# A two-layer hybrid decoder trunk: order of evacuations, last x sums and value transposes around a gated recurrence, and the place of one convolved tile

## The chip, the cores and the metric

The kernel runs on 1 core of one Trainium2 chip, as one launch. The time is device microseconds of that core; lower is better. The engines are TensorE (PE, with its weight loads PEld), VectorE (DVE), ScalarE (ACT), GpSimd (POOL) and SyncE (SP, which issues most DMAs). Each works through its own instructions in order; semaphores make one wait for another. Matmuls write to PSUM banks of 128x512 float32; DVE or ACT must empty a bank before it is used again.

## The reference

Input x is 1024 tokens by 1024 features, float32. Layer 0 mixes tokens with a gated linear recurrence (HGRN2, 8 heads of 128); layer 1 with sliding-window attention. Each layer then has a gated FFN (2816 wide) with a causal depthwise convolution of width 3, and layer norms after each part.

```python
q, f, i, g = split(h @ w_in, 4)
fg = lb + (1 - lb) * sigmoid(f)                 # forget gate; k = 1 - fg, v = i
o  = hgrn2_chunkwise(silu(q), 1 - fg, i, log(fg))   # S_t = diag(f_t) S_{t-1} + k_t v_t^T ; o_t = S_t^T q_t
o  = rmsnorm(o) * g_norm_w * silu(g)
h  = layer_norm(ALPHA * h + o @ w_out)
u  = causal_conv3(h @ ffn_w_in) + conv_b        # per channel
a, b = split(u, 2)
h  = layer_norm(ALPHA * h + (silu(a) * b) @ ffn_w_out)
```

## The kernel before

**Precision and products.** Every large matmul works on float32 split in two parts, hi (an ACT cast, L249, L874, L1298) and lo (a DVE subtraction, `low_part`, L197): hi x hi, hi x lo, lo x hi, the three matmuls of `mm3` (L222 to L224). Large products are cut by Strassen's scheme with seven products and sums of blocks of the weights and of x. A product here is 12 matmuls of 128x512 (four k blocks times three).

**The order.** PE's order, and in the recurrence that of ACT, DVE and SP too, is the order in which the program issues. `Order` (called `od`) keeps a model clock `od.t`, which each matmul advances, and a model of DVE's backlog, `od.v`. Side work is written as generators: `od.spawn(task, delay)` sets one up, `od.tick()` after each k block runs those whose time has come, `yield t` pauses one, `od.behind(us, least)` is the pause until DVE's backlog is done, and `od.finish` runs tasks to their end at once. A tick also calls a hook that issues weight casts on ACT (`cast_next`), and a filler that issues low parts on DVE (`job_next`).

**The recurrence.** Head 0's q, f, i and g are projected first; `ig_block` computes values and gates of row blocks tb = 4 to 7 (`tp` 2 and 3). Then `line` lists 98 products (m, p): pair m = 0 to 13 stands for head h = 1 to 7 and g = 0 (its q and f) or g = 1 (its gates and values), p is the Strassen product. A block of the line reads (m,1), (m-1,3), (m-1,4), (m,6), (m,5), (m,2), (m,7). The line starts with (0,1), (0,2), (0,6), (0,5), (0,7) and ends with (13,7), (13,3), (13,4). `product(n)` makes weights ahead, issues the 12 matmuls with a tick behind each of the four k blocks, and then spawns and steps `evacuate`, which empties the bank: p = 1, 6, 5 and 4 by an ACT copy (L1380, L1382, L1384, L1386), p = 2, 7 and 3 by a DVE add (L1392) and then an activation. Four banks serve the line: 1 for p = 2, 2 for p = 5 and 3, and 0 or 3 (by m's parity) for the others, so (13,4) uses the bank of (13,7).

**x sums.** The right operands of some products are sums of x's blocks. Those of product p = 5 are written by `last_sums(0)` over T's first four k blocks, columns 512 and up, which `ig_block` reads; its four row blocks each take an ACT cast (L874) and a DVE low part (L197). It is spawned after the last i/g block and finished before product (0,5). `opened` says how far along the line weights may be cast.

**The chain.** `all_heads` runs `recur(h)` for head after head: seven doubling levels (`update`, L1116 and L1118) with bursts of small matmuls into `psax` tiles (two of them, two banks each), `put`s that copy the scores to A; then k is transposed to kd (ACT copy L1187), and, for h > 0, the head's values, which the line leaves transposed, are turned by eight transposes and an ACT copy (L1196); then the state updates KV = kd, V (into psax), the states St on DVE, and the outputs. The chain waits until `values_in[0]` has reached h, which `evacuate` sets with (m,4) of g = 1. `norm` follows per head (L1235, L1239, L1248).

**The FFN.** `Up.run` goes over 22 columns fc of the up-projection, each with seven products. `collect` adds them up in Y, and for p = 4 and p = 3 runs the convolution of the a and b half: ACT writes the scaled u into a tile c (L526), DVE adds two shifted terms (L528, twice), and then c of the a half goes through SiLU (L531) and the b half is multiplied in (L533; on POOL for fc < 2, on DVE after) and stored to `gd`. The tile of the a half is row 4 or 5 of Y, that of the b half row 6 (Y6). `weight_load` (L471) brings a column's raw weights as two tiles r1 and r2 from a ring; for fc = 3 the second, r2, is row 7 of Y (Y7), as for each second column from then on. `weight_sums` makes sums of them (L480 to L483) and splits them (L249, L197). In the FFN only PE's order is the program's; the others are placed by the framework's scheduler, which keeps all dependences in program order: a load into a tile waits for earlier users of that tile.

## Time and profile before

| | us |
|---|---|
| median of 3 runs | 2119.31 |
| lowest, highest | 2119.15, 2119.46 |
| the profiled execution | 2119.05 |
| its span, first to last instruction | 2117.3 |
| PE busy in it | 2087.5 |
| DVE, ACT, POOL busy | 1777.7, 972.3, 189.0 |
| mean granted TensorE clock | 0.996 |

The recurrence's line of products runs from 63.1 to 435.9 us of the span, the first columns of layer 0's FFN from 554.6, those of layer 1's from 1490.9.

How to read the rows: a timeline row is start, duration, engine, line of the program, operation, tiles written<-read, shape, count, and in brackets the engine's idle time before it and what ended it. A row of waits is the engine with the waiting tile and line, what it waited for, the total, the number and the longest. A window's row is its bounds and length, busy time and count of PE, PEld, DVE, ACT, POOL, then the clock granted to TensorE (1.00 is full), the share of the DMA engines that was busy, and GB/s. PE's matmuls overlap, so their rows last longer than their distance.

### The profile page before, as it was taken

The numbers are of one execution on the slowest core, as the hardware profiler recorded it, in microseconds if no ns is written. First come the engines' busy times: TensorE is split into PE (matmuls) and PEld (weight loads), VectorE is DVE, ScalarE is ACT, GpSimd is POOL, SyncE is SP. The second block draws the span as 40 slices with busy tenths as digits, with TensorE's granted clock in tenths as the row PEclk, the third lists the DMA queues.
The fourth block names the chain that finished last, engine by engine and source line by source line (L and its number), as shares of the span: only waits on it lengthen the run. The fifth ranks groups of instructions, "written<-read, shape, count | busy, mean of one in ns | idle before, by whom it ended". The sixth has DMA issues, their size and how long they took to land. (4 is left out here: it accounts for less than half of the span.)

```text
span 2117.3 us, 31595 instructions
## 1 busy us (share of the span) xinstructions
PE 2087.5 (99%) x12303; PEld 1737.2 (82%) x12303; DVE 1777.7 (84%) x2420; ACT 972.3 (46%) x1586; POOL 189.0 (9%) x214
## 2 busy tenths in 40 slices
PE   9899999999999999999999999999999999999998
PEld 8688888877878888888888888888888888888886
DVE  6777777759989989887988668979999999978986
ACT  6555655543444444443533366743544444444430
POOL 1000000001010000000001122311010000000002
PEclk9999999999999999999999999999999999999999
DMA  4021111333247765628754511052266776449662
GB/s 153 21 70 51 51 51 51 100 135 109 90 124 183 185 163 149 160 93 297 261 189 159 159 35 37 24 159 91 88 169 165 176 178 160 120 154 325 224 207 100
DMA packets 239823, 286.82 MB, mean 135 GB/s; under 512 B 30216, under 2 KB 160440, under 8 KB 239416
## 3 DMA queue, kind: packets, MB, share of 16 engines
q1 hardware_dynamic: 223360, 238.26, 34.8%
q0 software_dynamic: 15456, 46.16, 11.0%
q8 instruction: 97, 1.59, 0.3%
q14 instruction: 54, 0.44, 0.1%
q10 hardware_dynamic: 856, 0.37, 0.1%
HBM read 241.72 MB, written 89.15 MB: 156 GB/s over the span
## 5 line engine op out<-in xcount | busy, mean ns | idle before, releaser
L222 PE MATMUL psmm<-T,HL 128*128 128x512 f32 x816 | 323.4, 396 | 7.9 <-ACT T L874 4.8
L223 PE MATMUL psmm<-T,HL 128*128 128x512 f32 x816 | 319.4, 391 | 1.2 <-DVE T L197 1.2
L224 PE MATMUL psmm<-T,HL 128*128 128x512 f32 x816 | 319.3, 391 | 0.2 <-DVE HL L197 0.2
L528 DVE SCALAR_TENSOR_TENSOR Y<-Y,cwt,Y 128x1023 f32<-128x1023 f32 (+1 forms) x176 | 225.2, 1281 | 50.8 <-ACT Y L526 49.4
L249 ACT CAST HL<-rx 128x1024 fp32r<-128x1024 f32 (+1 forms) x151 | 151.3, 1007 | 164.1 <-PE psmm L223 29.0
L197 DVE TENSOR_TENSOR HL<-rx,HL 128x1024 fp32r<-128x1024 f32 (+1 forms) x151 | 176.4, 1175 | 16.5 <-ACT HL L249 16.3
L222 PEld LDWEIGHTS psmm<-T,HL 128*128 128x128 f32 x816 | 153.9, 189 | 40.3 <-ACT T L874 5.2
L224 PEld LDWEIGHTS psmm<-T,HL 128*128 128x128 f32 x816 | 153.9, 189 | 33.0 <-DVE HL L197 0.6
L223 PEld LDWEIGHTS psmm<-T,HL 128*128 128x128 f32 x816 | 154.1, 189 | 32.8 <-DVE T L197 2.2
L222 PE MATMUL psax<-T,HL 128*128 128x512 f32 x392 | 152.9, 390 | 0.0
L223 PE MATMUL psax<-T,HL 128*128 128x512 f32 x392 | 152.6, 389 | 0.0
L224 PE MATMUL psax<-T,HL 128*128 128x512 f32 x392 | 152.5, 389 | 0.0
L526 ACT ACTIVATE Y<-Y,cwt 128x1024 f32<-128x1024 f32 x88 | 108.8, 1237 | 93.5 <-DVE Y L515 83.5
L197 DVE TENSOR_TENSOR HL<-raw,HL 128x512 fp32r<-128x512 f32 (+1 forms) x121 | 92.3, 789 | 45.7 <-ACT HL L1298 35.6
L271 POOL TENSOR_TENSOR rs<-rs,nhalf 128x1 f32<-128x1 f32 x32 | 45.0, 1406 | 735.7 <-DVE rs L270 735.7
L249 ACT CAST HT<-rx 128x1024 fp32r<-128x1024 f32 (+1 forms) x37 | 35.5, 960 | 135.0 <-DVE rx L482 67.4
L222 PE MATMUL psmm<-HL 128*128 128x512 f32 x220 | 86.6, 394 | 0.0
L222 PEld LDWEIGHTS psax<-T,HL 128*128 128x128 f32 x392 | 73.7, 188 | 15.3 <-DVE Y L509 0.2
L224 PEld LDWEIGHTS psax<-T,HL 128*128 128x128 f32 x392 | 73.6, 188 | 15.4
L223 PEld LDWEIGHTS psax<-T,HL 128*128 128x128 f32 x392 | 73.5, 188 | 15.1
L224 PE MATMUL psmm<-HL 128*128 128x512 f32 x220 | 85.7, 390 | 0.0
L223 PE MATMUL psmm<-HL 128*128 128x512 f32 x220 | 85.7, 390 | 0.0
(404 smaller groups left out, 5194.7 us busy)
## 6 DMA issues: line engine op xcount, KB each, us to landing
rx<-in_ffn_w_in_dram SPq DMA_DIRECT2D x136, 256.0 KB
rx<-gd SPq DMA_DIRECT2D x118, 256.0 KB
bsd<-in_ffn_w_out_dram POOLq DMA_DIRECT2D x36, 768.0 KB, 8.6
gd<-Y SPq DMA_DIRECT2D x44, 512.0 KB
raw<-in_hgrn_w_in_dram SPq DMA_DIRECT2D x30, 512.0 KB
rx<-in_ffn_w_out_dram SPq DMA_DIRECT2D x54, 256.0 KB
R<-bsd SPq DMA_DIRECT2D x44, 256.0 KB
Y<-in_ffn_w_in_dram SPq DMA_DIRECT2D x40, 256.0 KB
```

The lines of the kernel that those rows point to most:

```text
L197: make = lambda e: e.tensor_tensor(lo, src, hi.bitcast(F32), op=ALU.subtract)
L222: nc.tensor.matmul(ps, st(0), mv(0), start=start, stop=False, skip_group_check=onto)
L223: nc.tensor.matmul(ps, st(0), mv(1), start=False, stop=False, skip_group_check=onto)
L224: nc.tensor.matmul(ps, st(1), mv(0), start=False, stop=stop, skip_group_check=onto)
L249: nc.scalar.copy(hi, src)
L271: nc.gpsimd.tensor_tensor(rs, rs, nhalf, op=ALU.pow)
L526: nc.scalar.activation(c, u, AF.Identity, bias=cwt[:, l, 3, ci:ci + 1], scale=cwt[:, l, 2, ci:ci + 1])
L528: nc.vector.scalar_tensor_tensor(c[:, sh:], u[:, :S - sh], cwt[:, l, 2 - sh, ci:ci + 1], c[:, sh:], op0=ALU.mult, op1=ALU.add)
```

## The change

- `collect`: for fc = 1 the convolved tile of the b half is Y7; for all others it stays Y6.
- `ig_block` takes a callback, and the last x sums are spawned row block by row block, each behind the i/g block that last reads its part of T. `opened` is set to the whole line after the first product.
- `product`: the tick behind a product's last k block comes after the first step of that product's evacuation. For pair 0 the activation behind a DVE add pauses 5.0 at least, where it paused 0.8.
- `recur`: the values are no longer turned in the chain; the pause behind kd is 2.6 (2.0 for the last two heads), where it was 2.8. `turn_values(h)` does it as a task of its own, 3.0 behind the evacuation of the values' last part, and sets `values_in`.

```diff
--- before.py
+++ after.py
@@ -522,7 +522,7 @@
                 part = 0 if p == 4 else 1
                 ci = fc + part * NF
                 u, ca = C[:, part, :], Y[:, 4 + fc % 2, :]
-                c = Y[:, 6, :] if part else ca
+                c = Y[:, 7 if fc == 1 else 6, :] if part else ca
                 nc.scalar.activation(c, u, AF.Identity, bias=cwt[:, l, 3, ci:ci + 1], scale=cwt[:, l, 2, ci:ci + 1])
                 for sh in (1, 2):
                     nc.vector.scalar_tensor_tensor(c[:, sh:], u[:, :S - sh], cwt[:, l, 2 - sh, ci:ci + 1],
@@ -772,7 +772,7 @@
             nc.scalar.copy(vg[:, 0], pv[:, :, 0, :])
             yield 0.0
 
-        def ig_block(h, us, tp, ahead=None):
+        def ig_block(h, us, tp, ahead=None, behind=None):
             if ahead:
                 ps = psmm()
                 first_rows(us, ps, ahead)
@@ -788,6 +788,8 @@
                     od.tick()
                 soon.append(od.spawn(values(tb, ps)))
                 gated.setdefault(h, []).append(soon[-1])
+                if behind:
+                    behind(tb)
                 od.tick()
 
         def soon_all(left=0):
@@ -864,9 +866,9 @@
                 low_part(t[:, 1], src, t[:, 0], None)
                 od.vec(0.7)
 
-        def last_sums(part):
-
-            for i in range(4):
+        def last_sums(part, blocks=range(4)):
+
+            for i in blocks:
                 ts = slice(i * P, (i + 1) * P)
                 t, src = (TXs[1][:, :, :, ts], xf[i][:, 512:]) if part else (
                     T[:, :, :4, 512 + i * P:512 + (i + 1) * P], s1[:, i])
@@ -1185,16 +1187,10 @@
             put()
             kd = hp.tile([P, S], F32, name="kd")
             nc.scalar.copy(kd, ps)
-            yield 2.8
+            yield 2.6 if h < NH - 2 else 2.0
             while values_in[0] < h:
                 yield 0.2
             V = VG[h][:, 0, :].rearrange("p (c d) -> p c d", c=NB)
-            if h:
-                ps = psax()
-                for c in range(NB):
-                    tr(ps[:, c * P:(c + 1) * P], V[:, c, :])
-                nc.scalar.copy(VG[h][:, 0, :], ps)
-                yield 2.2 if h < NH - 2 else 1.3
             ps = psax()
             for c in range(NB - 1):
                 cs = slice(c * P, (c + 1) * P)
@@ -1218,6 +1214,15 @@
                     mm32(ps[:, cs], qp[:, cs], St[:, c, :], start=False)
             values_done[0] = h
             normed.append(od.spawn(norm(h, ps.rearrange("p (c t) -> p c t", c=NB))))
+
+        def turn_values(h):
+
+            ps = psax()
+            for c in range(NB):
+                tr(ps[:, c * P:(c + 1) * P], VG[h][:, 0, c * P:(c + 1) * P])
+            nc.scalar.copy(VG[h][:, 0, :], ps)
+            values_in[0] = h
+            yield 0.0
 
         def norm(h, pv):
 
@@ -1384,7 +1389,7 @@
                 nc.scalar.copy(second[:, late], ps)
             elif p == 4 and g:
                 nc.scalar.copy(first[:, late], ps)
-                values_in[0] = h
+                od.spawn(turn_values(h), 3.0)
             elif p == 4:
                 forget(h, first, kp, late, ps)
             else:
@@ -1392,7 +1397,7 @@
                 tt(to[:, half], to[:, half], ps, op=add)
                 od.vec(0.7)
                 taken.append(1)
-                yield od.behind(0.1, 0.8)
+                yield od.behind(0.1, 0.8 if m else 5.0)
                 if p != 2:
                     nc.scalar.activation(to[:, half], to[:, half], AF.Silu)
                 elif g == 0:
@@ -1414,12 +1419,14 @@
             for k in range(4):
                 od.t += 0.031
                 mm3(ps, lambda j: w[:, j, k * P:(k + 1) * P], lambda j: moving[p](j, k), k == 0 and p in (1, 2, 5), k == 3, onto=p in (6, 7, 3, 4))
-                od.tick()
+                if k < 3:
+                    od.tick()
             done[0] = n + 1
             taken = []
             readers[b] = od.spawn(evacuate(m, p, ps, taken)), taken
             evacs.setdefault(m, []).append(readers[b][0])
             od.step(readers[b][0])
+            od.tick()
 
         values_done, normed = [-1], []
         wo = a["hgrn_w_out"][0]
@@ -1486,17 +1493,17 @@
                     yield from recur(h, *args)
 
             task = od.spawn(all_heads(), 0.5)
+            firsts = []
             for tp in range(2, 4):
-                ig_block(0, us, tp)
-            opened[0] = len(line)
-            firsts = od.spawn(last_sums(0), 0.2)
+                ig_block(0, us, tp, behind=lambda tb: firsts.append(od.spawn(last_sums(0, [tb - 4]), 0.1)))
             soon_all()
             banks = [psmm() for _ in range(4)]
             lead, moved = 1, []
             for n, (m, p) in enumerate(line):
                 if m == 0 and p == 5:
-                    od.finish([firsts])
+                    od.finish(firsts)
                 product(n)
+                opened[0] = len(line)
                 h, g = pairs[m]
                 if n == 90:
                     od.finish(evacs[12])
```

## The prediction

> **What bounds the kernel now.** I read the page first, then the waits of TensorE, then the windows around its longest waits, then the timeline of each engine there.

> ```profile
> span 2117.3 us, 31595 instructions
> PE 2087.5 (99%) x12303; PEld 1737.2 (82%) x12303; DVE 1777.7 (84%) x2420; ACT 972.3 (46%) x1586; POOL 189.0 (9%) x214
> ```

> TensorE is the bound nearly everywhere, so an edit is worth exactly the waits of TensorE that it takes away, plus what follows them. The waits are few:

> ```profile
> PE psmm L222 <- ACT T L874: 4.8, 1, 4.8
> PE psmm L224 <- DVE HL L197: 2.9, 2, 2.7
> PE psmm L222 <- DVE VG L1392: 2.7, 1, 2.7
> PE psax L228 <- ACT VG L1196: 2.0, 5, 0.7
> ...
> PE psmm L222 <- ACT fg L1380: 1.0, 1, 1.0
> ...
> PE psax L232 <- ACT A L1097: 0.4, 1, 0.4
> ```

> The columns are the total in us, the number of waits, the longest. Each of the four largest lies where one part of the change works: the last x sums (L874), the second FFN weight block (the 2.7 of L197), the bank of the last head's values (L1392) and the values turned in the chain (L1196).

> A wait costs more than its length. These windows stand just behind the three long ones; the last columns are the granted clock, the DMA share and GB/s:

> ```profile
> 80.20:85.50 5.30, 4.86 (x13) 3.58 (x14) 1.18 (x2) 0.53 (x2) 0.00 (x0) 0.60 0.00 0
> 431.40:436.00 4.60, 4.49 (x13) 3.53 (x14) 0.65 (x2) 1.68 (x2) 0.00 (x0) 0.63 0.91 357
> 609.50:613.60 4.10, 4.03 (x11) 3.18 (x12) 4.10 (x6) 1.43 (x2) 0.00 (x0) 0.58 0.87 254
> ```

> The clock fell to about 0.6. At full clock one 128x512 step takes 0.225 us (two neighbours, below, start 0.22 apart), so 13 steps are 2.9 and 11 are 2.5: lost are 2.4, 1.7 and 1.6 us. [...] The two waits of 2.7 show the same fall, and the measurement decides.

> **(a) Last x sums per row block: about -7.8.** Product (0,5) needs four row blocks of T, each one ACT cast and one DVE low part. Before, the casts begin after the last i/g block; two of the four run behind the chain's copies, which wait for DVE.

> ```profile
> 66.69 0.60 ACT L874 CAST T<-VG 128x512 fp32r<-128x512 f32 x1
> ...
> 75.35 0.62 ACT L1103 COPY kd<-qp 128x512 f32<-128x512 f32 x1 [4.98 <-DVE qp L1116]
> ...
> 78.61 0.60 ACT L874 CAST T<-VG 128x512 fp32r<-128x512 f32 x1
> 79.12 0.57 ACT L1382 COPY qs<-psmm 128x512 f32<-128x512 f32 x1
> ```

> ```profile
> 79.47 1.91 DVE L197 TENSOR_TENSOR T<-VG,T 128x512 fp32r<-128x512 f32 x3
> ```

> ```profile
> 80.26 0.80 PE L222 MATMUL psmm<-T,HL 128*128 128x512 f32 x1 [4.80 <-ACT T L874]
> ```

> After, the cast of a block is issued as its i/g product ends, all ahead of where the first now stands, and the low parts (0.64 us each, 1.91 for three) go to DVE in the modelled gaps of its queue. That is 2.6 us of DVE ahead of the first score burst, of which three quarters stood behind it so far. It pushes back the chain, and for none of the chain's bursts does TensorE wait here. Gone are 4.80 and the clock's 2.4; also the 1.0 for fg, because the first bank's copy is now issued ahead of the weight casts that `opened` let in. Together 8.2. Those casts come one product later and are wanted from (0,7) on, three products after: hidden. Late next is product (0,7), whose bank waits for the copy at 79.12. With (0,5) from 80.26-4.80=75.5 it starts 12x0.225=2.7 later, at 78.2. The copy stands behind the chain's two (75.35 plus twice 0.62 gives 76.6): done at 77.2, free, if the three activations that now fill 76.6 to 78.6 come after it. The 5.0 us pause for pair 0 puts them there; if not, 1.0 is lost. I take 0.4. Bounds -8.2 and -5 (two blocks still late).

> **(b) Banks first: about -4.0.** The last product's bank was freed late:

> ```profile
> 425.88 0.69 DVE L1116 TENSOR_TENSOR qp<-qp,tot 128x512 f32<-128x512 f32 x1
> ...
> 430.74 1.30 DVE L1392 TENSOR_TENSOR VG<-VG,psmm 128x512 f32<-128x512 f32 x2
> ```

> ```profile
> 422.10 0.39 PE L224 MATMUL psmm<-HL 128*128 128x512 f32 x1
> ...
> 428.17 0.39 PE L223 MATMUL psmm<-Y,HL 128*128 128x512 f32 x1
> 428.39 0.39 PE L224 MATMUL psmm<-Y,HL 128*128 128x512 f32 x1
> ```

> (13,7) ends its matmuls at 422.5, its add could run then, but was queued behind a chain step that filled DVE from 425.88 to 430.7. Issued first it is done by about 423.2, and (13,4) follows (13,3) at 428.6: gained are 2.7+1.7=4.4. Against it, an add at the head of DVE's queue makes the chain wait until its product ends; but the list of waits names hardly a bank beside this and fg's, so the products hide it and I cost it at nothing. If a shorter chain puts that step a product earlier, the add stands behind it again and the gain is 0. I take -4.0.

> **(c) Values turned outside the chain: about -1.6.** The eight transposes and the ACT copy stay, at another place; the 2.0 and the 0.4 of waits go. KV now waits for kd alone, after a pause of 2.6:

> ```profile
> 143.38 1.09 PE L232 MATMUL psax<-ident,kp 128*128 128x128 f32 x8
> ...
> 293.03 1.09 PE L232 MATMUL psax<-ident,kp 128*128 128x128 f32 x8
> ```

> ```profile
> 148.25 1.01 ACT L1187 COPY kd<-psax 128x1024 f32<-128x1024 f32 x1
> ...
> 294.21 1.01 ACT L1187 COPY kd<-psax 128x1024 f32<-128x1024 f32 x1 [0.30 <-PE psax L232]
> ```

> From the end of the transposes to the end of the copy are 295.22-294.12=1.1 us in head 4, covered, and 149.26-144.47=4.8 in head 1, where up to 2.2 would show. I give back 0.8. The turn also takes one of the two psax tiles outside the chain's order; the trace of before cannot show what that costs. The nearest row is the 0.4 of L1097, a tile that was not free once: between 0 and 7x0.4=2.8, and I take 0, since that head's copies were late for the same reason as kd. Bounds -2.4 and -2.4+2.2+2.8=+2.6.

> **(d) The second convolved tile in Y7: about +2.4.** Before, both first columns convolve into Y6; ACT waits for POOL's multiply and DVE for ACT:

> ```profile
> 594.43 1.24 ACT L526 ACTIVATE Y<-Y,cwt 128x1024 f32<-128x1024 f32 x1 [3.35 <-POOL Y L533]
> ```

> ```profile
> 595.71 1.28 DVE L528 SCALAR_TENSOR_TENSOR Y<-Y,cwt,Y 128x1023 f32<-128x1023 f32 x1 [2.97 <-ACT Y L526]
> ...
> 608.29 1.22 DVE L197 TENSOR_TENSOR HL<-Y,HL 128x1024 fp32r<-128x1024 f32 x1
> ```

> That low part released TensorE at 609.5, after the 2.7. Take away DVE's 2.97 and it ends at 606.5, where TensorE wants it: -2.7 and the clock's 1.6. But Y7 is also where column 3's second raw weights land, early:

> ```profile
> 559.05 1.16 SPq L471 DMA_DIRECT2D Y<-in_ffn_w_in_dram  x2
> ```

> ```profile
> 590.63 3.77 POOL L533 TENSOR_TENSOR Y<-Y 128x1024 f32<-128x1024 f32 x1 [42.86 <-DVE Y L528]
> 598.96 2.41 POOL L533 TENSOR_TENSOR Y<-Y 128x1024 f32<-128x1024 f32 x1 [4.56 <-DVE Y L528]
> ```

> Now this load, on SP's queue, must wait until POOL has read Y7: at the earliest 594.40+2.41=596.8, with POOL's slower multiply 598.2. From issue to landing:

> ```profile
> 609.54 0.92 SPq L471 DMA_DIRECT2D Y<-in_ffn_w_in_dram  x2
> ...
> 1573.71 2.12 SPq L471 DMA_DIRECT2D Y<-in_ffn_w_in_dram  x1
> ```

> ```profile
> 614.13 0.62 ACT L249 CAST HL<-Y 128x512 fp32r<-128x512 f32 x1 [0.95 <-DMA Y<-in_ffn_w_in_dram]
> ...
> 1582.30 0.62 ACT L249 CAST HL<-Y 128x512 fp32r<-128x512 f32 x1 [3.27 <-DMA Y<-in_ffn_w_in_dram]
> ```

> 4.6 and 8.6 us. Then three sums, a cast and a low part:

> ```profile
> L482 DVE TENSOR_TENSOR Y<-Y,rx x20: 683/692/2614, 599.3 to 1853.1; 128x512 f32<-128x512 f32 x20
> ```

> Alone 3x0.69+1.24+1.22=4.5 (the cast at double the 0.62 of 512 columns); with DVE as crowded as from 599.3 to 609.5 it is 10.2+1.4=11.6. I take 5.5, near the lower end because DVE comes to this stretch 2.97 earlier. Layer 0: 598.2+4.6+5.5=608.3 against the 609.5 of now, -1.2. Layer 1 runs the same code, and there TensorE did not wait:

> ```profile
> 1543.06 0.39 PE L224 MATMUL psmm<-TX,HL 128*128 128x512 f32 x1
> ```

> ```profile
> 1530.02 1.25 ACT L526 ACTIVATE Y<-Y,cwt 128x1024 f32<-128x1024 f32 x1 [1.98 <-POOL Y L533]
> ```

> ```profile
> 1535.42 2.40 POOL L533 TENSOR_TENSOR Y<-Y 128x1024 f32<-128x1024 f32 x1 [5.44 <-DVE Y L528]
> ```

> POOL ends at 1537.8, less the 1.98 that ACT no longer waits: 1535.8+4.6+5.5=1545.9, a wait of 2.8 and half the clock's price, 0.8, since 2.7 is the shortest wait seen to pay it. Sum +2.4. Behind the load on SP stand those of later columns, wanted a column (84 steps, 19 us) later: hidden. Bounds: -4.3 (no wait in either layer) and, with 8.6 and 11.6, 618.4-609.5=9 plus 1556.0-1543.1+1.6=14.5. [...]

> **Sum.** -7.8-4.0-1.6+2.4=-11.0. The profiled execution took 2119.05 (span 2117.3 and 1.75 around it), the median is 2119.31, 0.26 above; the same difference on the median gives 2108.3.

> **The rivals.** *Y7 costs nothing:* the load lands in time in both layers, (d) is -4.3 and the time 2101.6. For it: 4.4 us of work against DVE's 2.97 won. Against: at the earliest 596.8+4.6+4.5=605.9 is in time in layer 0, but 1535.8+4.6+4.5=1544.9 is not in layer 1.
> *The chain changes its phase:* each head's chain is shorter by transposes of 1.09 and a pause of 2.2, so its DVE steps meet other products, and (b) and (c) come to nothing: -7.8+2.4 gives 2113.9; with (a) at its -5 as well, 2116.7. For it: the whole gain of (b) hangs on which step lies behind (13,7). Against: hardly a bank but that one was late.
> *Slower, by the Y7 load:* in both layers it lands after 8.6 us and its sums are spread as before, +9 and +14.5 against -13.4 from the rest: 2129.4. It decides when the two layers together lose over 17.6, some 9 each. For it: SP issues the two gd stores at the same time. Against: DVE is freer then.

> **How the numbers follow.** A measurement of this kernel can tell 0.2%, 4.2 us: faster means under 2115.1. Forecast 0.48 (its own range 2104 to 2113), Y7 free 0.21, phase 0.22, of which 0.09 still faster and 0.13 within 0.2%, slower 0.09. So faster 0.78, same 0.13, slower 0.09. The range 2101 to 2117 leaves out the slower rival and about a tenth at the edges of the others.

> **What would show it.** (a) No wait of (0,5) on L874, and a clock of 1.00 between 75 and 86. (b) No wait on L1392 at the line's end. (c) No ACT copy of values before KV; a wait for kd, if any, in head 1. (d) Y6's 3.35 gone; the load into Y7 issued only behind POOL's second multiply, and a wait of TensorE on HL L197 in both layers, the one in layer 1 new. I am wrong if new waits stand among the other products, or if layer 1 shows none.

## The result and the profile after

The changed kernel takes 2128.72 us (median of 6 runs, 2127.38 to 2129.66) where the kernel before took 2120.00 on the same chip (6 runs): a ratio of 1.004, 95% interval 1.0027 to 1.0053. It is slower by 8.7 us, where 11.0 less was forecast. The profiled execution took 2129.32 (span 2127.5).

First the waits of TensorE in the changed kernel: who waited for whom, and then the total in us, how many times, the longest.

```profile
PE psmm L222 <- ACT HL L249: 10.1, 2, 5.3
PE psax L228 <- ACT kd L1189: 6.0, 3, 2.8
PE psmm L224 <- DVE HL L197: 2.5, 3, 1.8
```

The 4.8 on T, the 2.7 on the late bank, the 2.0 on the turned values and the 1.0 on fg, which the prediction wanted gone, are gone. In their place stand two large new ones: 10.1+2.5 on HL, all but 0.2 of it in the feed-forward layers, and 6.0 on kd, in the recurrence.

The layers can be measured apart, since each starts with the same instruction. From the start of the first product of layer 0 (the first matmul into psax from T and HL) to that of layer 1, and from there to the end, the traces give (in the kernel before it starts at 541.9 and 1478.3, in each layer 12.6 ahead of the mark given further up):

| kernel | line's first product to layer 0 | layer 0 to layer 1 | layer 1 to the end |
|---|---|---|---|
| before | 478.8 | 936.3 | 639.0 |
| changed | 475.2 | 940.4 | 648.5 |

Single executions differ: three kernels that are alike up to layer 0 gave 475.2, 477.2 and 474.2 for the first column. The eight executions here whose layers have the code of before gave 934.7 to 937.6 for the second and 638.3 to 639.7 for the third. So the recurrence won 3.6 of the 13.4 forecast for it, layer 0 lost 4.1 (a gain of 1.2 was forecast), and layer 1 lost 9.5 (3.6 was forecast). Layer 1 is the plainest place to read. POOL's second multiply, the load into Y7 behind it on SP, and what DVE, ACT and TensorE then do, in the timeline of the changed kernel (start, duration, engine, line; in brackets the idle time before and who ended it):

```profile
1531.53 3.22 POOL L533 TENSOR_TENSOR Y<-Y 128x1024 f32<-128x1024 f32 x1 [1.25 <-DVE Y L528]
```

```profile
1535.28 1.19 SPq L471 DMA_DIRECT2D Y<-in_ffn_w_in_dram  x2
```

```profile
1538.73 0.69 DVE L480 TENSOR_TENSOR rx<-Y,rx 128x512 f32<-128x512 f32 x1 [0.18 <-DMA Y<-in_ffn_w_in_dram]
1539.34 1.28 DVE L528 SCALAR_TENSOR_TENSOR Y<-Y,cwt,Y 128x1023 f32<-128x1023 f32 x1
1540.53 1.22 DVE L518 TENSOR_TENSOR Y<-Y,psmm 128x1024 f32<-128x1024 f32 x1
1541.66 1.28 DVE L528 SCALAR_TENSOR_TENSOR Y<-Y,cwt,Y 128x1022 f32<-128x1022 f32 x1
...
1544.06 0.69 DVE L481 TENSOR_TENSOR Y<-Y 128x512 f32<-128x512 f32 x1
...
1546.99 0.69 DVE L482 TENSOR_TENSOR Y<-Y,rx 128x512 f32<-128x512 f32 x1
...
1550.52 1.22 DVE L197 TENSOR_TENSOR HL<-Y,HL 128x1024 fp32r<-128x1024 f32 x1
```

```profile
1548.81 0.80 PE L222 MATMUL psmm<-TX,HL 128*128 128x512 f32 x1 [5.32 <-ACT HL L249]
1551.80 0.80 PE L224 MATMUL psmm<-TX,HL 128*128 128x512 f32 x1 [1.77 <-DVE HL L197]
```

The first half of the load lands 3.4 us after its issue, where the prediction took 4.6 for the whole. But of the three sums that need it (L480, L481, L482) the last begins only 8.3 us later, and the low part ends at 1551.74, 13.0 after the landing, where the prediction took 5.5. DVE isn't waiting in between: the three sums and the low part are 3.3 of the 13.0, and in the rest its order of work has the convolution (L528), the collecting adds (L518) and other low parts between one sum and the next. TensorE waits 5.32 for the high part and 1.77 for the low part. Layer 0 is alike: issue at 596.45, the first sum at 601.21, the low part's end at 609.58, 8.4 after it. (There DVE was busy up to the first sum, so the load may have landed before.)

In a table of stretches (busy time and count of TensorE, the granted clock, the share of the DMAs and GB/s), layer 0 and layer 1 of the changed kernel, the waits and the four microseconds behind each:

```profile
602.90:610.00 7.10, 1.76 (x4) 0.83 0.18 74
610.00:614.00 4.00, 4.00 (x10) 0.50 0.72 207
1543.30:1552.00 8.70, 1.61 (x4) 0.67 0.27 88
1552.00:1556.50 4.50, 4.50 (x11) 0.50 0.68 215
```

Behind each wait the clock is at 0.50 for four microseconds or more; that is the rest of the loss, about 2 us a layer (half of 4.0 and of 4.5), of which the kernel before paid 1.6 in layer 0 too.

### The profile page after: what moved, and what is told of

It is laid out like the page before. It is cut to its first block, busy times and chain, and to the rows that moved or that the text cites. A ratio compares the mean times of both kernels' runs of the same rounds, so it can differ in the third digit from the quotient of the medians.

```text
span 2127.5 us, 31578 instructions
## 1 busy us (share of the span) xinstructions
PE 2091.0 (98%) x12303; PEld 1742.4 (82%) x12303; DVE 1777.9 (84%) x2420; ACT 970.5 (46%) x1586; POOL 189.1 (9%) x214
## 4 chain that ended last, share of the span: by engine, by line
PE 68%; DVE 3%; DMA 0%; issue 0%; ACT 0%; POOL 0%; SPq 0%; DVEq 0%; POOLq 0%; ACTq 0%
PE psmm L224 13%; PE psmm L222 12%; PE psmm L223 12%; PE psax L222 9%; PE psax L224 9%; PE psax L223 9%; PE psmm L228 1%; PE psax L1695 1%; PE psmm L232 1%; DVE Y L528 1%; DVE HL L197 0%; PE psax L232 0%; DMA rx<-in_ffn_w_in_dram 0%; DMA Y<-in_ffn_w_in_dram 0%; DVE TX L197 0%
## 5 line engine op out<-in xcount | busy, mean ns | idle before, releaser
L222 PE MATMUL psmm<-T,HL 128*128 128x512 f32 x816 | 322.4, 395 | 0.5 <-DVE VG L758 0.4
L223 PE MATMUL psmm<-T,HL 128*128 128x512 f32 x816 | 318.3, 390 | 0.9 <-DVE T L197 0.9
L224 PE MATMUL psmm<-T,HL 128*128 128x512 f32 x816 | 318.5, 390 | 0.2 <-DVE HL L197 0.2
L528 DVE SCALAR_TENSOR_TENSOR Y<-Y,cwt,Y 128x1023 f32<-128x1023 f32 (+1 forms) x176 | 226.7, 1290 | 47.3 <-ACT Y L526 45.8
L249 ACT CAST HL<-rx 128x1024 fp32r<-128x1024 f32 (+1 forms) x151 | 151.0, 1006 | 175.4 <-DMA rx<-in_ffn_w_in_dram 44.7
L197 DVE TENSOR_TENSOR HL<-rx,HL 128x1024 fp32r<-128x1024 f32 (+1 forms) x151 | 177.1, 1179 | 25.2 <-ACT HL L249 25.0
L224 PEld LDWEIGHTS psmm<-T,HL 128*128 128x128 f32 x816 | 153.3, 188 | 32.7 <-DVE HL L197 0.6
L222 PEld LDWEIGHTS psmm<-T,HL 128*128 128x128 f32 x816 | 153.4, 188 | 31.9 <-DVE VG L758 0.7
L223 PEld LDWEIGHTS psmm<-T,HL 128*128 128x128 f32 x816 | 153.5, 188 | 31.6 <-DVE T L197 1.3
L222 PE MATMUL psax<-T,HL 128*128 128x512 f32 x392 | 153.4, 391 | 0.0
L224 PE MATMUL psax<-T,HL 128*128 128x512 f32 x392 | 152.7, 390 | 0.0
L223 PE MATMUL psax<-T,HL 128*128 128x512 f32 x392 | 152.7, 390 | 0.0
L526 ACT ACTIVATE Y<-Y,cwt 128x1024 f32<-128x1024 f32 x88 | 108.8, 1237 | 91.4 <-DVE Y L515 91.4
L197 DVE TENSOR_TENSOR HL<-raw,HL 128x512 fp32r<-128x512 f32 (+1 forms) x121 | 92.3, 790 | 38.0 <-ACT HL L1303 27.0
L249 ACT CAST HT<-rx 128x1024 fp32r<-128x1024 f32 (+1 forms) x37 | 35.5, 959 | 125.2 <-DVE rx L482 48.4
L222 PE MATMUL psmm<-HL 128*128 128x512 f32 x220 | 86.5, 393 | 0.0
L223 PEld LDWEIGHTS psax<-T,HL 128*128 128x128 f32 x392 | 74.0, 189 | 15.3
L222 PEld LDWEIGHTS psax<-T,HL 128*128 128x128 f32 x392 | 73.9, 189 | 15.1
L224 PEld LDWEIGHTS psax<-T,HL 128*128 128x128 f32 x392 | 73.6, 188 | 15.3
L224 PE MATMUL psmm<-HL 128*128 128x512 f32 x220 | 85.8, 390 | 0.0
L223 PE MATMUL psmm<-HL 128*128 128x512 f32 x220 | 85.8, 390 | 0.0
```

The costliest lines, as they stand in the source:

```text
L197: make = lambda e: e.tensor_tensor(lo, src, hi.bitcast(F32), op=ALU.subtract)
L222: nc.tensor.matmul(ps, st(0), mv(0), start=start, stop=False, skip_group_check=onto)
L223: nc.tensor.matmul(ps, st(0), mv(1), start=False, stop=False, skip_group_check=onto)
L224: nc.tensor.matmul(ps, st(1), mv(0), start=False, stop=stop, skip_group_check=onto)
L249: nc.scalar.copy(hi, src)
L526: nc.scalar.activation(c, u, AF.Identity, bias=cwt[:, l, 3, ci:ci + 1], scale=cwt[:, l, 2, ci:ci + 1])
```

## The experiments

Each was timed against the kernel before on the same chip, whose medians lay between 2119.5 and 2120.2.

**The Y7 edit apart.** First the changed kernel without it, then the kernel before with nothing else.

```diff
-                c = Y[:, 7 if fc == 1 else 6, :] if part else ca
+                c = Y[:, 6, :] if part else ca
```

> The changed kernel with the second convolved tile of column 1 back in Y6, so that the load into Y7 has nobody to wait for. Theory (the Y7 edit costs some 14 us over both layers, the recurrence gains some 6): 2113 to 2115 us, TensorE's waits on HL L249 and HL L197 in layer 1 gone, layer 0 as in the kernel before. Rival (the layers' new waits come from the recurrence's new phase, in which TensorE reaches them earlier): 2124 to 2129, the waits stay.

Measured: 2115.09 us, ratio 0.9974 (0.9964 to 0.9983); from layer 0 to layer 1 936.7, to the end 638.3, as before. The waits on HL are gone from layer 1; layer 0 has one of 3.1, as the kernel before had one of 2.7.

> The kernel before with the Y7 edit alone. Theory: the recurrence is as before and both layers lose as in the changed kernel, 2131 to 2135 us. Rival (the edit is harmless at the old phase, or wins its 3 us on ACT): 2116 to 2121.

Measured: 2132.90 us, ratio 1.0062 (1.0048 to 1.0076); 941.2 and 648.8. The waits of TensorE on ACT's HL in layer 0 and layer 1 of this kernel:

```profile
PE psmm L222 <- ACT HL L249: 4.9, 1, 4.9
...
PE psmm L222 <- ACT HL L249: 5.1, 1, 5.1
```

They are those of the changed kernel, without any of the recurrence's edits. So the Y7 edit costs 13.6 us in company (2128.7-2115.1) and 12.9 alone (2132.9-2120.0): it is additive, and the rival of a new phase falls.

**A place that nobody else wants.** Column 1's collected tile C has two halves; once the first is convolved it is free until column 3 collects into it, a column later.

```diff
-                c = Y[:, 7 if fc == 1 else 6, :] if part else ca
+                c = (C[:, 0, :] if fc == 1 else Y[:, 6, :]) if part else ca
```

> The changed kernel with the second convolved tile in column 1's own collected tile, whose first half is free by then: it is apart from Y6 and Y7. Theory: neither the wait of ACT for POOL nor the late load, so 1 to 4 us under the kernel with Y6: 2109 to 2114 us. Rival (the stalls come from the place being another one at all, by DVE and POOL overlapping more, or from the phase): above 2120.

Measured: 2110.90 us, ratio 0.9960 (0.9947 to 0.9972); 933.3 and 638.7. Against the kernel with Y6 it wins 4.2 us, and its trace has 3.5 of that in layer 0 (936.7 to 933.3) and none in layer 1. POOL's second multiply in layer 0, here and with Y6:

```profile
590.33 2.39 POOL L533 TENSOR_TENSOR Y<-Y,Y 128x1024 f32<-128x1024 f32 x1 [1.25 <-DVE Y L528]
```

```profile
597.82 2.39 POOL L533 TENSOR_TENSOR Y<-Y 128x1024 f32<-128x1024 f32 x1 [4.56 <-DVE Y L528]
```

And the stretch round the wait, the place of its own first, Y6 second:

```profile
600.00:616.00 16.00, 14.78 (x65) 1.00 0.53 163
```

```profile
600.00:616.00 16.00, 12.89 (x50) 0.89 0.38 131
```

With the second tile apart from Y6 the multiply comes 7.5 us earlier, 3.3 of which is the earlier start of the layer in this execution (537.1 against 540.4). The wait on the low part falls from 3.1 to 1.2 and the clock behind it stays at 1.00. That is what the edit could win, and the -4.3 that the prediction gave for a Y7 without a cost. What decided was who else wanted the place.

**The pause ahead of kd's products.** With the second tile in Y6, the chain waits longer after the copy of kd before it issues what reads it.

```diff
-            yield 2.6 if h < NH - 2 else 2.0
+            yield 5.0 if h < NH - 2 else 3.3
```

> The changed kernel with Y6 and with the pause between the cast of kd and the products that read it at 5.0 (3.3 in the last two heads) in place of 2.6 (2.0). Theory: the waits on kd of heads 0, 1 and 4 (2.8+2.9+0.8, less what is late next) are the pause being too short for ACT's queue: 4 to 6 us under the kernel with Y6 alone, 2107 to 2110. Rival (the chain is the bound there and the lost time comes up elsewhere, since a longer pause pushes each head's end back): within 2 us of the kernel with Y6 alone, or slower.

Measured: 2146.29 us, ratio 1.0125 (1.0111 to 1.0138): 31 us slower than with 2.6. The theory missed altogether; its rival had the direction, not the size. The waits on kd went down from 6.3 to 2.9, but the transposes of og of head 6 hold up TensorE for 16.2 us:

```profile
444.04 1.97 PE L232 MATMUL psax<-ident,og 128*128 128x128 f32 x8 [16.21 <-DVE og L1244]
```

DVE's multiply waits 9.34 for POOL's factors, POOL for ACT's squares (the last ends at 440.73, POOL begins at 440.81), and the squares stand in ACT's queue behind a cast for the output projection that waits for a load of finished heads:

```profile
435.82 1.04 ACT L1462 CAST T<-fg 128x1024 fp32r<-128x1024 f32 x1 [14.19 <-DMA fg<-hod]
```

The pauses sum to 17.0 more; how much of the 31 us is the chain being later by that, and how much the cast ahead of the squares, these runs don't part. A longer pause is no remedy in any case.

> The changed kernel with the second tile in column 1's own collected tile (2110.9) and the pause ahead of the products that read kd by head: 5.0, 5.0, 1.6, 1.6, 3.4, 1.6, 2.0, 2.0, which is 2.6 more over all heads than 6 x 2.6 + 2 x 2.0, where pauses of 5.0 and 3.3 had added 17. Theory (the pause of 2.6 is too short for ACT's queue in heads 0, 1 and 4 and longer than need be in the others, and what a longer pause had cost is the chain's end in the last head): waits on kd under 1.5 in all and no wait of head 7's transposes on og, 2105 to 2109 us. Rival (any longer pause comes back whole at the chain's end, there is no slack): 2110 to 2114, with a wait at the end of 2 or more.

The edit is on the kernel with C's half:

```diff
-            yield 2.6 if h < NH - 2 else 2.0
+            yield (5.0, 5.0, 1.6, 1.6, 3.4, 1.6, 2.0, 2.0)[h]
```

Measured: 2118.11 us, ratio 0.9988 (0.9978 to 0.9997), 7 slower than with 2.6. There is no wait at the chain's end, but two of 3.7 and 3.9 on kd stand in heads 2 and 3, whose pause was 1.6 and which had not waited with 2.6. Both sides missed: in these heads 1.6 is short of what stands ahead of kd. In head 5 the same 1.6 brings no wait.

**What stands ahead of kd's copy.** ACT in the changed kernel, head 0, in the timeline; TensorE has ended the transposes of kp, behind which the copies of A and kd come, at 90.5:

```profile
90.20 0.59 ACT L1385 COPY VG<-psmm 128x512 f32<-128x512 f32 x1
90.81 1.67 ACT L1303 CAST HL<-raw 128x512 fp32r<-128x512 f32 x3
92.39 0.63 ACT L1402 ACTIVATE qs<-qs 128x512 f32<-128x512 f32 x1
92.92 1.12 ACT L1303 CAST HL<-raw 128x512 fp32r<-128x512 f32 x2
93.94 0.74 ACT L1099 COPY A<-psax 64x256 f32<-64x256 f32 x2
94.71 1.01 ACT L1189 COPY kd<-psax 128x1024 f32<-128x1024 f32 x1
```

Five casts of weights and a Silu, from 90.81 to 93.94, stand in ACT's queue ahead of two copies that could have begun at 90.8, when ACT's copy before them ends. On the kernel with C's half, none is given to ACT while kd is on its way:

```diff
+            hook, od.hook = od.hook, None
             yield wait
             put = blocks(6, chunks(psax()), early, early)
...
             nc.scalar.copy(kd, ps)
+            od.hook = hook
             yield 2.6 if h < NH - 2 else 2.0
```

> The changed kernel with the second tile in column 1's own collected tile (2110.9), and no casts of weights given to ACT between the chain's transposes of kp and its copy of kd. Theory (what the copy of kd waits for is ACT's queue, three casts and a Silu given to it just ahead): waits on kd 2.5 or less in all, 2104 to 2108 us. Rival (it waits for the chain's own copies, or the phase shifts and the time comes up elsewhere): 2110 or more.

Measured: 2107.18 us, ratio 0.9942 (0.9929 to 0.9956), the best kernel of the study. ACT of this kernel in head 0, and its wait on kd:

```profile
90.66 0.62 ACT L1305 CAST HL<-raw 128x512 fp32r<-128x512 f32 x1
91.18 0.63 ACT L1404 ACTIVATE qs<-qs 128x512 f32<-128x512 f32 x1
91.71 0.73 ACT L1099 COPY A<-psax 64x256 f32<-64x256 f32 x2
92.47 1.01 ACT L1190 COPY kd<-psax 128x1024 f32<-128x1024 f32 x1
93.38 2.18 ACT L1305 CAST HL<-raw 128x512 fp32r<-128x512 f32 x4
```

```profile
PE psax L228 <- ACT kd L1190: 2.9, 3, 1.8
```

kd is copied 2.2 us earlier than in the changed kernel, four casts come behind it, and the waits on kd fall from 6.2 to 2.9; the time falls by 3.7. So half of the wait was ACT's queue of casts; what the other half stands behind wasn't tried. (The bound of 2.5 was missed by 0.4.)

> The same kernel (2110.9) with the pause of 0.8 in place of 5.0 ahead of the first pair's Silus. Theory (the Silu that stands ahead of kd's copy in head 0 was put there by this pause): head 0's wait on kd falls by 0.6 or more, 2108 to 2111 us. Rival (the pause keeps ACT free for the last sums): a wait on T comes back, 2112 to 2116.

The edit is `yield od.behind(0.1, 0.8)` in place of `0.8 if m else 5.0`. Measured: 2110.85 us, ratio 0.9961 (0.9949 to 0.9974), kd's waits 6.0 in all and 2.8 at the longest, no wait on T. The pause does nothing that shows either way; the Silu ahead of kd's copy isn't its doing, and neither side has what it expected but the number.

**The recurrence's parts.** The code of a part is that of the change's diff. The banks alone:

```diff
-                od.tick()
+                if k < 3:
+                    od.tick()
...
             od.step(readers[b][0])
+            od.tick()
```

> The kernel before with the banks emptied first, alone. Theory of the prediction (the late bank of product (13,7) and the clock behind it are won): the wait of 2.7 on the bank gone, 2115 to 2117 us. Rival (the chain meets other products and a wait comes up elsewhere): 2119 to 2122.

Measured: 2119.17 us, ratio 0.9996 (0.9987 to 1.0005). The wait of 2.7 on the bank is gone, but of this kernel's waits in the recurrence and the output projection two are longer and two are new:

```profile
PE psax L228 <- ACT VG L1196: 2.9, 5, 0.8
PE psmm L232 <- DVE Y L380: 2.3, 1, 2.3
PE psmm L222 <- ACT T L249: 1.0, 1, 1.0
PE psmm L1537 <- DVE HL L197: 1.0, 1, 1.0
```

The first was 2.0 and the second 1.3 before: 3.9 us came where 2.7 and its clock had gone, most of it behind the line, at the output projection and the norm after it. The clock fell there too, to 0.50 from 517.3 to 520.6, where it had been full before.

The same lines taken back from the kernel with C's half:

> The same kernel (2110.9) without the banks emptied first: sums per block and values outside the chain alone. Theory now (alone this part was worth 1 at most, so it does nothing here either): 2109 to 2113 us. Prediction's (it wins 4.0): 2114 to 2117.

Measured: 2111.47 us, ratio 0.9968 (0.9955 to 0.9980), against 2110.90 with the banks first. In company, too, they are worth nothing that shows.

The values alone:

```diff
-            yield 2.8
+            yield 2.6 if h < NH - 2 else 2.0
...
-            if h:
-                ps = psax()
-                for c in range(NB):
-                    tr(ps[:, c * P:(c + 1) * P], V[:, c, :])
-                nc.scalar.copy(VG[h][:, 0, :], ps)
-                yield 2.2 if h < NH - 2 else 1.3
...
-                values_in[0] = h
+                od.spawn(turn_values(h), 3.0)
```

> The kernel before with the values turned outside the chain and the shorter pause, alone. Theory now (2.4 of waits go and some 3.7 on kd come in heads 1 and 4): 2119 to 2122 us. Prediction's (the waits on kd cost 0.8): 2117 to 2119.

Measured: 2119.75 us, ratio 0.9997 (0.9988 to 1.0006); its waits on kd are 1.0 in all, the 2.0 on VG are gone, and 1.5 on a bank (`VG L1383`) and 1.5+1.1 at the output projection are new. The interval, -2.8 to 1.3 us, holds the prediction's -1.6 and also nothing. The wait on kd is 0.8's size, but it stands in head 0 (at 99.9), not in head 1, where the prediction had it.

The sums taken back from the kernel with C's half (the blocks of last_sums, opened, and the pause of 5.0):

> The same kernel (2110.9) without the last x sums per block: banks first and values outside alone. Prediction's (the sums are worth 7.8): 2117 to 2120 us, with the wait of 4.8 on T back. Rival (the waits on kd of heads 0 and 1 come from the earlier start that the sums bring, and most of the gain goes there): 2111 to 2115.

Measured: 2120.86 us, ratio 1.0007 (0.9998 to 1.0016): the sums are worth 10.0 in company (2120.9-2110.9), the wait of 4.8 on T is back. The waits on kd are 2.3 in this kernel and 6.2 with the sums, so the rival had a part of it, but the sums win far more than they give back there.

Not all of the 10.0 is the sums' own, though. The kernel without them has a long wait at the line's end that the kernel with them (2110.9) does not have:

```profile
PE psax L232 <- ACT VG L1221: 4.7, 1, 4.7
```

The last head's transposes of kp want a psax tile. `turn_values` holds it until ACT copies the turned values, at 444.51, behind four casts and two activations; TensorE goes on at 445.57, with the clock at 0.50 from 443.9 to 450.7. So the banks and the values without the sums didn't win the 5.6 forecast for them: 2120.9 stands against 2119.5 for the kernel before, although C's half, worth some 4 beside the other parts, is in it.

And the sums with the banks on the kernel before, so without the values and the Y7 edit:

> The kernel before with the last x sums per row block and the banks emptied first, but the values turned in the chain and the second tile in Y6. Theory (the wait on kd in head 0 comes with the sums, whose casts and later Silus stand ahead of it on ACT; those of heads 1 and 4 come with the values): head 0's wait of some 2.8 stays, those of heads 1 and 4 go, the waits on VG come back: 2112 to 2115 us against 2115.1 with the values outside too. Rival (all waits on kd come with the values' part): no wait on kd, 2108 to 2111.

Measured: 2129.82 us, ratio 1.0048 (1.0035 to 1.0060), slower than all of it by 14.7 (2115.1) and slower than the kernel before. Neither side expected that. The waits of TensorE in the recurrence of this kernel:

```profile
PE psax L228 <- ACT VG L1198: 6.8, 6, 3.8
PE psax L232 <- ACT A L1099: 6.7, 5, 2.0
PE psax L232 <- DVE og L1241: 2.0, 1, 2.0
PE psax L228 <- ACT kd L1189: 1.9, 1, 1.9
```

In five heads the transposes of the values wait for ACT's copy of A, and in six (two of them make up most of the 6.8) the products of kd and the values for ACT's copy of the turned values: two chain copies a head behind ACT's queue, where the kernel before waited 2.0+0.4 for them in the whole line. Its chain takes 52.8 us a head (from the column sums of head 1 to those of head 7, over 6), the kernel before 49.2, the changed kernel 49.7. With the values turned outside the chain both of these waits are gone.

The sums alone, without the banks or the values, were not tried.

**Held casts elsewhere.** Is it the casts in that kernel too?

The hold of above on the kernel before, and then on sums and banks alone:

> The kernel before with no casts of weights given to ACT between the chain's transposes of kp and its copy of kd, alone. Theory (ACT's queue ahead of the chain's copies costs time where the chain waits for them, which in the kernel before is only some 2.4 in all): 2117 to 2120 us. Rival (shorter queues help the chain everywhere): below 2115.

Measured: 2120.83 us, ratio 1.0007 (0.9998 to 1.0016). No gain where the chain hardly waits.

> Sums per block and banks first with the values turned in the chain (2129.8), with the casts held. Theory (the waits of the turn on ACT's copies of A, 6.7 in five heads, are the queue of casts ahead of them): those waits under 3, 2120 to 2125 us. Rival (the phase of the chain against the products; the evacuations, not the casts, stand ahead): 2127 to 2131.

Measured: 2130.51 us, ratio 1.0049 (1.0035 to 1.0063): no gain, the rival's number. But the waits moved:

```profile
PE psax L228 <- ACT VG L1200: 14.7, 6, 5.0
...
PE psax L232 <- ACT A L1099: 0.7, 2, 0.5
```

6.7 on A became 0.7, and 6.8 on VG became 14.7. ACT in head 2, between the copies of kd and of the turned values:

```profile
196.27 1.01 ACT L1190 COPY kd<-psax 128x1024 f32<-128x1024 f32 x1
197.18 0.64 ACT L1401 ACTIVATE qs<-qs 128x512 f32<-128x512 f32 x1
197.71 2.17 ACT L1302 CAST HL<-raw 128x512 fp32r<-128x512 f32 x4
199.78 0.63 ACT L1401 ACTIVATE qs<-qs 128x512 f32<-128x512 f32 x1
...
202.40 0.99 ACT L1200 COPY VG<-psax 128x1024 f32<-128x1024 f32 x1
```

The casts that were held ahead of kd come out behind it, ahead of the next copy that the chain needs, with Silus and the gates' activations besides: 5.1 us between the two copies. In the kernel with the values outside there is no such copy behind kd, which fits that the same hold wins there. Theory and rival both had half: the wait is ACT's queue, but with two copies in the chain the queue only changes which one waits.

And the best kernel without the banks first:

> Sums per block, values outside the chain, second tile in column 1's own collected tile, casts held, banks not first. Theory (the banks first are worth nothing): 2106 to 2109 us, as with them (2107.2). Rival (worth its 4 once the chain waits less): 2110 to 2112.

Measured: 2108.95 us, ratio 0.9948 (0.9935 to 0.9960), against 2107.18 with the banks first: 1.8 us, less than the measurement tells. The banks stay worth little.

## Why the prediction was wrong

**The step that failed: "I take 5.5, near the lower end because DVE comes to this stretch 2.97 earlier"** (part d). The chain of that part was right link by link: the load can be issued only behind POOL's second multiply, Y6's wait of ACT for POOL goes, TensorE waits on HL in both layers. The term between landing and the low part's end measured 8.4 (from the first sum) in layer 0 and 13.0 in layer 1. The row for it was in hand, and stood in the prediction as a bound: in the kernel before the same stretch, spread among DVE's other work, gave 10.2+1.4=11.6. The rows above show DVE busy throughout, with the sums at their places between the convolution's steps. Its being earlier by 2.97 shifted that work and did not thin it. Worked with 11.6 in both layers, the prediction's own sum gives 598.2+4.6+11.6=614.4, +4.9, and 1535.8+4.6+11.6=1552.0, 8.9 late and the clock's 1.6, +10.5: together 15.4 in place of 2.4, where 13.6 (4.1+9.5) was measured. That term alone turns the forecast from -11.0 to +2.0. The rest of the miss lies in the recurrence, by parts (b) and (c) below: it won 3.6 where 13.4 had been forecast.

In layer 0 the rest of the difference was small: the issue was at 596.45 with the layer's start 3.4 earlier than before, so at 599.85 on the old time where 598.2 had been worked out.

**The clock** was mis-sized in layer 1: 0.8 was taken for a wait of 2.8, and the wait of 7.1 cost 2.2 (4.5 us at 0.50). In layer 0 the prediction's sum leaves a wait of 1.5 (608.3 against 606.8) and yet credits nothing of the clock's 1.6, though it holds 2.7 for the shortest wait that pays; by its own rule (d) would have been +0.8 and the forecast -12.6, farther off. And the 1.7 that part (b) adds to the bank's wait of 2.7 is a chance: the kernel with Y7 alone has the same wait, at 433.39, and 1.00 granted behind it.

**Part (a), the sums**, was right in its mechanism: no wait on T, 1.00 granted between 71.7 and 86. Its size is not so well shown: in the 10.0 us in company against 7.8, the 4.7 at the line's end and the clock behind it count for the sums, and 3.9 more on kd (6.2-2.3) count against them.

**Part (b), the banks**, failed by the rival's reason: -4.0 was forecast, some -0.8 (the ratio of 0.9996, within its interval nothing) and -0.6 were measured. The bank's wait did go, and others came, most of them behind the line, at the output projection and the norm after it, which the prediction hadn't costed.

**Part (c), the values**, agrees alone in its number and is wrong in company, in both directions. That it agrees is in part luck, since the wait of 1.0 on kd isn't the one that was costed. The wait for kd was named, but with 0.8 in head 1 alone; beside the sums it is 6.0 in heads 0, 1 and 4, and 1.7 of clock behind head 0's in the profiled execution (below). The cause that the runs show, for half of it, is ACT's queue: the prediction counted the pause and TensorE's cover, not the casts that ACT is given meanwhile. The psax tile that the turn takes out of the chain's order was costed at 0, within 0 to 2.8; without the sums it cost 4.7 and the clock behind it. What the prediction could not see, since no row of the kernel before had it, is that the sums with the banks would make the turn in the chain a wait in most heads, so that taking it out is worth 14.7 there.

**The rivals.** "Slower, by the Y7 load" gave 2129.4, and 2128.72 was measured, but not by its sum: it wanted the layers to lose 23.5 against a gain of 13.4, and they lost 13.6 against a gain of 3.6 in the profiled executions (4.9 by the kernel with Y6, 2120.0-2115.1). "The chain changes its phase" had the recurrence at -7.8 or -5.0, the nearest to those, and was right that (b) comes to nothing. Both happened together. The prediction held them as alternatives, though one lies in the recurrence and the other in the layers, and had no case with both.

## What to carry to other kernels

When a tile gets another place, ask who writes that place next and from when, and price the new wait to its far end: not landing plus the work alone, but landing plus the work as the engine's order spreads it, for which the same stretch in the profile of before has a row. An engine that is off the critical path by its busy time can still be on it by its queue: what counts is what is given to it just ahead of the copy that the chain needs, and moving that out of the way (3.7 us here) or taking a copy out of the chain (14.7 beside the other parts) pays where a longer pause costs (31 us for 17.0 of pauses). The copy that was taken out still holds its tile until it has run, and that can become the next wait (4.7 us here). Parts of a change to one schedule don't add up; the Y7 edit, in another stage than the rest, did, within 1 us (13.6 and 12.9).

## What the runs showed of the hardware

```profile
95.77 3.35 PE L228 MATMUL psax<-VG,kd 128*128 128x128 f32 x14 [2.55 <-ACT kd L1189]
```

```profile
95.70:100.00 4.30, 4.23 (x19) 0.61 0.88 246
```

and with C's half:

```profile
95.06 1.83 PE L228 MATMUL psax<-VG,kd 128*128 128x128 f32 x14 [2.55 <-ACT kd L1189]
```

```profile
95.70:100.00 4.30, 4.30 (x26) 1.00 0.79 233
```

In one execution 1.7 us of clock (4.3 at 0.61) are lost behind the wait, in the other none. The traces of the kernel before and of the changed one have both kinds too. Their waits of TensorE of 1.2 us or more, with the stretch in which the clock stood at 0.50:

| kernel | the wait ends at | its length | clock at 0.50 | for |
|---|---|---|---|---|
| before | 80.26 | 4.80 | 77.64 to 84.46 | 6.82 |
| before | 431.51 | 2.73 | 432.62 to 436.03 | 3.41 |
| before | 515.76 | 1.29 | none, 1.00 to 518.0 | 0 |
| before | 609.57 | 2.69 | 610.12 to 613.53 | 3.41 |
| changed | 95.77 | 2.55 | 95.62 to 99.03 | 3.41 |
| changed | 148.27 | 2.77 | none, 1.00 to 152.3 | 0 |
| changed | 511.14 | 1.91 | 512.05 to 515.46 | 3.41 |
| changed | 607.83 | 4.76 | 607.62 to 614.45 | 6.83 |
| changed | 1548.81 and 1551.80 | 5.32 and 1.77 | 1546.29 to 1556.53 | 10.24 |

The 2.77 went free and the shorter 1.91 did not, so in these two traces the length alone doesn't tell which wait is paid for. What is paid shows in the layers too: with the second tile in Y6, layer 0 to layer 1 took 934.7 in the two executions that kept the clock behind the wait of 2.7 (values alone; sums and banks with casts held), and 936.3 to 937.6 in the six that didn't.

In layer 1 of the changed kernel POOL's second multiply (1531.53) took 3.22, where the two rows of layer 0 further up have 2.39, and the DVE instruction that began beside it

```profile
1533.02 2.28 DVE L197 TENSOR_TENSOR HL<-rx,HL 128x512 fp32r<-128x512 f32 x1
```

took 2.28, where one of this form took 0.69 alone (1543.45 in the same stretch). Two others were not longer: the low part that had begun 0.24 ahead of the multiply (1531.29) took 1.21, and the add from a PSUM bank (1532.42, L513) 0.68. By the difference of 3.22 and 2.39 the longer multiply put the issue of the load into Y7 back by 0.8 us, an estimate.
